# Modulation by row block, the input split from PSUM, and VectorE in place of GpSimd in a hybrid decoder layer

## The chip, the cores and the metric

The kernel runs on one core of a Trainium2 chip. The metric is device time in microseconds (us) of one launch. The engines are TensorE (PE, with its weight loads as PEld), VectorE (DVE), ScalarE (ACT), GpSimd (POOL) and SyncE (SP, which here only issues transfers).

## The reference, cut to what matters

One layer of a decoder with 1024 tokens and 1024 channels, all in float32:

```python
mod = (jax.nn.silu(c) @ w_ada + b_ada)[:, None, :]
shift, scale, gate = jnp.split(mod, 3, axis=-1)
h = rms_norm(x, norm_g) * (1.0 + scale) + shift
(a_q, a_kv, a_g, a_z, b_q, ..., d_z) = jnp.split(h @ w_in, IN_OFFSETS, axis=-1)
y_a = nsa_attention(...)           # three masked softmaxes per head, ALiBi slopes
y_b = banded_attention(...)        # window of 128, a sink per head
y_c = stick_breaking_attention(...)   # suffix sums of log(1 - sigmoid)
y_d = retention(...)
for i, (y, z) in enumerate(branches):
    yi = y.reshape(B, S, BRANCH_W) * jax.nn.silu(z)
    term = jax.nn.sigmoid(h @ w_merge[i]) * (yi @ w_br[i])
    merged = term if merged is None else merged + term
x = x + gate * (merged @ w_out)
return rms_norm(x, final_g)
```

## The kernel before, in words

**Exact products.** A float32 matrix product is made of three matmuls on parts: each operand is split into a high part (`whi`, `hh`, written by an ACT copy) and the rest (`wlo`, `hl`, a subtraction on DVE or POOL). TensorE sums hi*hi, hi*lo and lo*hi in PSUM.

**First stage** (`first_gen`). The eight 128-token tiles of x are loaded (`load_x`) and normalised (`norm_x`: squares and scaling on ACT, a small power on POOL). The shift and scale of the modulation are sums over the 1024 rows of `w_ada`. `load_ada(k)` loads for channel block k (128 channels) all 1024 rows of its shift and of its scale columns, 512 KB each, in pieces of 128 columns, thus 512 bytes each. `mod_k(k)` multiplies each of the eight row blocks by `silc`, which holds silu(c), and adds it up on DVE (`SP<-FA,silc,SP` or `SP<-SP,silc` in the trace, 256 columns an instruction). Two matmuls with a column of ones then sum over the partitions (`t<-SP`), and two small DVE steps write `mod`. `h_k(k, n)` transposes four x tiles into a PSUM bank `t`, has ACT apply scale and shift into a tile `xs` in SBUF (`t<-t,mod`; the pool of that tile is also named t1), has DVE copy it to `hh` and POOL subtract to `hl`. The first half of the tokens (`h0`) is done block by block, and each block's 18 matmuls (six products of `w_in` columns for mixer C, three parts each) follow; `w_in` comes in eight pieces of 384 KB, each split by ACT and POOL. The second half (`h1`) follows at the end. `WARM` is a run of 36 transposes without use for the result, ahead of the first matmuls.

**Mixers.** Units of attention C, D, A, B run between the projections. The softmaxes of A and B subtract a distance table with one DVE instruction that also takes the row's maximum (`mx`), multiply the maximum by the negative slope (`mx<-mx,kbt`), run the exponential on ACT with its row sum (`den`), clamp `den` by one DVE instruction over its two or four columns, invert it, and scale on POOL. Mixer C has a running sum on DVE (`TENSOR_TENSOR_SCAN`) whose unused second input is the tile it also reads first.

**Merge and output.** The gates of `w_merge` use a seven-product scheme on 2x2 blocks (`pair`, `product`, `op`), whose sums of `h` blocks (`td`, T1 to T3) are loaded back from DRAM into `tt`, six loads of 1 MB, ahead of the first two weight tiles' work. The output product uses the same scheme: `w_jobs` and the loops after it prepare the blocks of `w_out` (`wr`), in part on POOL, and write them over the blocks of `h` (`b11`, `b12`, `b21`, `b22`, in the trace `hh` and `hl`), over `yh` and `yl` (`wy`) and over `tt` (`w11`). The last block, `wt4`, takes memory that `wr` held.

**Order.** The instructions of each of four stretches (`with md.noted`) are collected and put in an order by a planner (`Program.schedule`): it simulates the engines with costs written in `cost`, and takes on each engine the ready step with the lowest rank. Tables (`SHIFT_PE`, `SHIFT`) move the rank of labelled steps. It also models that DVE and POOL steps flagged `port` exclude each other. The loops that prepare `b22`, `b12` and `wy` stand outside of the planned stretches. On the chip each engine runs its own list in that order.

All instructions issued through the planner have one line in the trace (L372); L395 marks those issued directly. Tiles are named by their pool: `SP` holds working rows (the modulation's sums, softmax rows), `FA` the x tiles and others, `wst` loaded weights, and PSUM banks are `d`, `s`, `t`, `y`.

Of the kernel before, what the change touches and what calls it, by code (L numbers as in the profile page):

```python
# [16 lines left out]
P = 128  # L17
S = 1024
# [27 lines left out]
def shape_constants():  # L46
# [14 lines left out]
    for h in range(NH):  # L61
        kb[:, KB_IS + h] = 1.0 / SLOPES[h]
# [26 lines left out]
def chunks(w):  # L89
# [22 lines left out]
    ('D1', 7): 19159, ('first', 0): 300, ('first', 2): 0, ('first', 3): 20000, ('first', 4): 3,  # L112
    ('first', 5): 9000, ('first', 6): 10000, ('first', 7): 10300, ('h0', 1): 9967, ('h0', 2): 1000,
    ('h0', 3): -300, ('h0', 4): 10030, ('h0', 5): -10000, ('h0', 6): 300, ('h0', 7): -10100,
    ('h1', 0): 30, ('h1', 1): -10000, ('h1', 4): 0, ('h1', 5): 10000, ('h1', 6): 19960,
    ('h1', 7): 113, ('item', 0): 397, ('item', 12): 19900, ('item', 15): -100, ('item', 16): 10570,
    ('item', 17): 18970, ('item', 19): 10170, ('item', 2): 10000, ('item', 20): 10000,
    ('item', 21): 20003, ('item', 22): 9970, ('item', 23): 10300, ('item', 24): -10,
    ('item', 25): 10013, ('item', 26): 830, ('item', 27): 9697, ('item', 4): -270,
    ('item', 6): -11000, ('item', 7): 10000, ('item', 9): 293, ('mod', 0): 10000, ('mod', 1): 0,  # L120
    ('mod', 4): 370, ('mod', 7): 300, ('out', 102): -10000, ('out', 103): 330, ('out', 106): -10030,
    ('out', 107): 10000, ('out', 109): 0, ('out', 110): 0, ('out', 111): 3000, ('out', 112): 9987,
    ('out', 113): 30, ('out', 114): 10000, ('out', 115): 10000, ('out', 117): -10,
    ('out', 119): -10890, ('out', 120): -30, ('out', 121): 3000, ('out', 122): -10000,
    ('out', 123): 10027, ('out', 124): 294, ('out', 126): -10800, ('out', 128): 10000,
    ('out', 129): 10000, ('out', 94): -407, ('out', 95): -3013, ('out', 96): 9900,
    ('out', 97): -130, ('tile', 0): 320, ('tile', 1): -570, ('tile', 10): -10010, ('tile', 11): 300,
    ('tile', 12): -990, ('tile', 13): 30, ('tile', 14): 3000, ('tile', 15): 10, ('tile', 16): 3000,
    ('tile', 17): 0, ('tile', 18): 10000, ('tile', 19): -9300, ('tile', 2): -100, ('tile', 21): 900,
# [19 lines left out]
    ('ada', 6): 20000, ('ada', 7): 0, ('first', 7): 0, ('h0', 0): 70, ('h0', 1): -9980,  # L149
    ('h0', 2): 12783, ('h0', 3): -7000, ('h0', 5): -1000, ('h0', 7): 0, ('h1', 0): -10000,  # L150
    ('h1', 1): -10000, ('h1', 2): 10200, ('h1', 5): 30, ('h1', 6): -33, ('item', 0): 0,
    ('item', 1): 0, ('item', 10): 400, ('item', 11): 2000, ('item', 12): 9882, ('item', 13): 0,
    ('item', 15): 0, ('item', 16): 320, ('item', 17): 10, ('item', 18): -333, ('item', 19): -10100,
    ('item', 2): 1330, ('item', 20): 20000, ('item', 21): -11000, ('item', 22): 0,
    ('item', 23): -30, ('item', 27): 0, ('item', 29): 30, ('item', 3): 1000, ('item', 30): 10000,
    ('item', 5): 0, ('item', 6): -307, ('item', 8): -200, ('mod', 0): -10000, ('mod', 2): -10130,
    ('mod', 3): 10, ('mod', 4): 300, ('mod', 5): -10930, ('mod', 6): -30, ('mod', 7): 0,
# [33 lines left out]
class Program:  # L191
# [127 lines left out]
    def schedule(self):  # L319
# [17 lines left out]
        while len(order) < len(ops):  # L337
# [89 lines left out]
def hybrid_kernel(ctx: ExitStack, tc: tile.TileContext, x, c, w_ada, b_ada, norm_g, w_in, cmp_pos,  # L427
# [567 lines left out]
    with ac:  # L995
# [101 lines left out]
        def first_gen():  # L1097
# [5 lines left out]
            for t in range(3):  # L1103
                load_x(t)
# [932 lines left out]
```

## Time and profile before

| | |
|---|---|
| median of 3 runs | 1100.29 us (1096.93 to 1100.64) |
| profiled execution | 1097.74 us, its span 1096.0 us |
| PE busy | 1041.4 us (95% of the span) |
| DVE, ACT, POOL busy | 821.6, 575.7, 490.8 us |
| mean granted clock of TensorE | 0.984 of full speed |
| PE busy share by 40 slices | 3 and 8 tenths in the first two, 9 in all others but the last (6) and two with 7 |

PE is busy nearly all the time, so the profile is read for the stretches in which it is not, and for those in which its granted clock (the column PEclk) is below 1.00; the two levels are 1.2 GHz (0.5) and 2.4 GHz (1.0).

### The profile page before, as it was taken

What the parts mean: (1) busy time and instruction counts of PE and PEld (TensorE: products, weight loads), DVE (VectorE), ACT (ScalarE), POOL (GpSimd) and SP (SyncE); (2) the same over time, 40 slices, a digit from 0 to 9 for tenths busy, and PEclk for the clock granted to TensorE, in tenths of its full rate; (3) what the DMA queues carried; (4) which work ended last, traced back from release to release, by engine and by line L of the source; (5) the groups of instructions that cost most, each with busy time, mean ns of one, the idle gap of its engine ahead of it and who ended that gap; (6) DMA issues with size and microseconds to landing.
All of it is one profiled execution on the core that took longest, in us unless ns stands there. A gap on an engine that the chain in (4) does not pass through costs nothing.

```text
span 1096.0 us, 16030 instructions
## 1 busy us (share of the span) xinstructions
PE 1041.4 (95%) x5391; PEld 874.2 (80%) x5391; DVE 821.6 (75%) x1803; ACT 575.7 (53%) x1265; POOL 490.8 (45%) x519
## 2 busy tenths in 40 slices
PE   3899999999999999999999899999999999997996
PEld 2688787789778888889888688888888888875885
DVE  5868995997467868988997345688796565589897
ACT  4378984896246767677775133333333333254343
POOL 4575214204444466564565122255555555485102
PEclk8899999999999999999999999999999999999998
DMA  9846211013232111232323912332232222261222
GB/s 306 243 134 180 68 39 39 16 26 78 32 78 59 30 49 41 90 110 88 99 85 129 344 49 85 99 94 70 87 87 58 53 79 79 69 232 43 111 98 94
DMA packets 127718, 105.47 MB, mean 96 GB/s; under 512 B 15132, under 2 KB 108372, under 8 KB 126868
## 3 DMA queue, kind: packets, MB, share of 16 engines
q1 hardware_dynamic: 126160, 99.95, 30.5%
q0 software_dynamic: 1408, 4.48, 1.3%
q8 instruction: 42, 0.69, 0.3%
q14 instruction: 40, 0.33, 0.1%
q10 hardware_dynamic: 68, 0.02, 0.0%
HBM read 81.88 MB, written 17.83 MB: 91 GB/s over the span
## 4 chain that ended last, share of the span: by engine, by line
PE 77%; DVE 10%; ACT 4%; DMA 4%; issue 2%; POOL 1%; SPq 1%; POOLq 0%; DVEq 0%; ACTq 0%
PE d L372 30%; PE s L372 22%; PE t L372 15%; PE y L372 9%; DVE SP L372 3%; DMA wst<-in_w_merge_dram 2%; ACT t L372 1%; DVE lo L372 1%; DVE FA L372 1%; ACT SP L372 1%; SPq L372 1%; DVE yl L395 1%; DMA SP<-in_w_ada_dram 1%; DVE acc L372 1%; DMA FA<-in_x_dram 1%
## 5 line engine op out<-in xcount | busy, mean ns | idle before, releaser
L372 POOL TENSOR_TENSOR wlo<-wst,whi 128x512 fp32r<-128x512 f32 (+1 forms) x108 | 145.2, 1354 | 175.3 <-ACT whi L372 173.4
L372 PE MATMUL d<-hh,whi 128*128 128x512 f32 x440 | 181.3, 412 | 1.7 <-ACT whi L372 0.7
L372 ACT ACTIVATE whi<-wst 128x512 fp32r<-128x512 f32 (+2 forms) x121 | 89.2, 740 | 161.2 <-PE s L372 42.7
L372 PE MATMUL d<-hh,wlo 128*128 128x512 f32 x440 | 173.2, 394 | 0.0
L372 PE MATMUL d<-hl,whi 128*128 128x512 f32 x440 | 172.2, 392 | 0.0
L372 PEld LDWEIGHTS d<-hh,wlo 128*128 128x128 f32 x440 | 82.9, 188 | 19.1 <-DVE wlo L372 0.4
L372 ACT ACTIVATE hi<-t 128x512 fp32r<-128x512 f32 (+3 forms) x148 | 74.9, 527 | 38.4 <-PE t L372 34.1
L372 PEld LDWEIGHTS d<-hh,whi 128*128 128x128 f32 x440 | 83.3, 189 | 14.3 <-ACT whi L372 1.1
L372 PEld LDWEIGHTS d<-hl,whi 128*128 128x128 f32 x440 | 83.1, 189 | 10.6
L372 DVE TENSOR_TENSOR lo<-t,hi 128x512 fp32r<-128x512 f32 (+2 forms) x132 | 80.6, 623 | 11.9 <-ACT hi L372 10.9
L372 POOL TENSOR_SCALAR SP<-SP,den,gates 128x640 f32<-128x640 f32 (+7 forms) x64 | 53.0, 837 | 75.1 <-DVE den L372 25.5
L372 PE MATMUL s<-hh,whi 128*128 128x512 f32 x200 | 79.8, 399 | 6.3 <-ACT whi L372 6.3
L372 POOL TENSOR_TENSOR acc<-acc,mt 128x512 f32<-128x512 f32 x44 | 67.2, 1528 | 34.4 <-DVE mt L372 33.6
L372 PE MATMUL s<-hh,wlo 128*128 128x512 f32 x200 | 79.1, 395 | 0.9 <-DVE wlo L372 0.9
L372 PE MATMUL s<-hl,whi 128*128 128x512 f32 x200 | 78.5, 394 | 0.0
L372 PE MATMUL t<-kbt,SP 128*128 128x128 f32 (+1 forms) x470 | 69.5, 273 | 7.4 <-DMA kbt<-in_kb_dram 6.5
L372 ACT ACTIVATE SP<-SP,mx 128x257 f32<-128x257 f32 (+9 forms) x96 | 62.2, 650 | 20.7 <-DVE mx L372 17.0
L372 PEld LDWEIGHTS t<-kbt,SP 128*128 128x128 f32 (+1 forms) x470 | 55.0, 141 | 14.7 <-DMA kbt<-in_kb_dram 6.5
L372 DVE TENSOR_TENSOR mt<-s,mt 128x512 f32<-128x512 f32 x61 | 41.2, 686 | 33.9 <-PE s L372 33.7
L372 PE MATMUL s<-tt,whi 128*128 128x512 f32 x192 | 59.1, 389 | 0.0
L372 ACT ACTIVATE mt<-mt 128x512 f32<-128x512 f32 x56 | 35.2, 630 | 41.4 <-DVE mt L372 41.2
L372 ACT ACTIVATE t<-t 128x512 f32<-128x512 f32 (+5 forms) x97 | 49.9, 523 | 3.7 <-DVE t L372 2.3
(347 smaller groups left out, 2798.3 us busy)
## 6 DMA issues: line engine op xcount, KB each, us to landing
wst<-in_w_merge_dram SPq DMA_DIRECT2D x32, 512.0 KB, 4.3
wst<-in_w_in_dram SPq DMA_DIRECT2D x26, 512.0 KB, 3.9
td<-FA SPq DMA_DIRECT2D x32, 256.0 KB, 2.5
tt<-td SPq DMA_DIRECT2D x6, 1024.0 KB, 12.6
FA<-in_w_ada_dram SPq DMA_DIRECT2D x10, 512.0 KB, 7.1
FA<-in_x_dram SPq DMA_DIRECT2D x8, 512.0 KB, 6.7
pst<-in_w_br_dram SPq DMA_DIRECT2D x32, 128.0 KB, 2.3
ga<-in_w_ada_dram SPq DMA_DIRECT2D x16, 256.0 KB, 3.0
```

The costliest lines, as they stand in the source:

```text
L372: fn(*args, **kw)
L395: return f(*a, **k)
```

## The change

**Modulation.** The eight channel blocks form three groups (blocks 0 and 1, 2 and 3, 4 to 7). A transfer brings one row block (128 rows) of one group, with pieces of 256 columns (1 KB) in the first two groups and 512 columns (2 KB) in the third, into a ring of six 4 KB rows; the loads of x tiles 0 to 3 alternate with those of group 0. DVE sums a group at a time (512 or 1024 columns an instruction), and all of a group's sums over partitions follow. x tiles 4 to 7 are loaded after the third group.

**Input parts.** ACT writes `hh` straight from PSUM and then the full value back to PSUM in a second pass; DVE subtracts from PSUM to `hl`. The copy on DVE and the subtraction on POOL are gone.

**Softmax and scan.** The slope enters in the instruction that takes the extreme (now a minimum of negated scores), so the multiplication of `mx` is gone; the clamp of `den` is one instruction for each column; the scan's second input is in PSUM.

**T loads and w_out.** T2 is loaded first, T3 and T1 after the first weight tile's matmuls were issued. All POOL subtractions of `w_out`'s blocks and of `wt4` are on DVE, and `b22`, `b12`, `wy` are inside the planned stretch.

**Planner.** It adds 88 ns when PE goes from transposes to matmuls. Both tables are new, save for the labels `out` from 102 on, nearly all of `op` from 107 on, and `wt4`.

```diff
+            op.turn |= name == "transpose"
...
+                free[e] += 88.0 * (turned and not op.turn)
+                turned = op.turn
...
+        MG = ((0, 2), (2, 4), (4, 8))
+        macc = [misc[:, 512:1024], misc[:, 512:1024], SP[:, 3, :]]
+        RING = [FA[:, 4], FA[:, 5], FA[:, 6], FA[:, 7], SP[:, 1], SP[:, 2]]
...
+        NEXT = {(0, 1): ((1, 4), (1, 5)), (0, 3): ((1, 6), (1, 7)), (0, 5): ((2, 0),), (0, 7): ((2, 1),), (1, 1): ((2, 2),),
+                (1, 3): ((2, 3),), (1, 5): ((2, 4),), (1, 7): ((2, 5),), (2, 0): ((2, 6),), (2, 1): ((2, 7),)}
...
-        def load_ada(k):
-            for s in range(2):
-                sy.dma_start(AD[k][:, s], w_ada[0].rearrange("(r p) c -> p r c", p=P)[:, :, s * D + k * P:s * D + (k + 1) * P])
+        def load_ada(g, r):
+            k0, k1 = MG[g]
+            sy.dma_start(AD[g, r], w_ada[0, r * P:(r + 1) * P, 0:2 * D].rearrange("p (s c) -> p s c", s=2)[:, :, k0 * P:k1 * P])
...
+        def mod_g(g):
+
+            k0, k1 = MG[g]
+            m = macc[g].rearrange("p (s c) -> p s c", s=2)
+            for r in range(KC):
+                md.label = "mod", 8 * g + r
+                if r == 0:
+                    ve.tensor_scalar(m, AD[g, r], silc[:, 0:1], None, op0=ALU.mult)
+                else:
+                    ve.scalar_tensor_tensor(m, AD[g, r], silc[:, r:r + 1], m, op0=ALU.mult, op1=ALU.add)
+                for gr in NEXT.get((g, r), ()):
+                    md.label = "ada", 8 * gr[0] + gr[1]
+                    load_ada(*gr)
...
-            xs = t1_pool.tile([P, 512], F32, name=f"xs{k}_{n}", tag="t1")
-            se.activation(xs, t, AF.Identity, scale=mod[:, 16 + k:17 + k], bias=mod[:, k:k + 1])
-            ve.tensor_copy(hh[:, k, sl], xs)
-            po.tensor_tensor(hl[:, k, sl], xs, hh[:, k, sl].bitcast(F32), ALU.subtract)
+            for d in (hh[:, k, sl], t):
+                se.activation(d, t, AF.Identity, scale=mod[:, 16 + k:17 + k], bias=mod[:, k:k + 1])
+            ve.tensor_tensor(hl[:, k, sl], t, hh[:, k, sl].bitcast(F32), ALU.subtract)
...
-                                ve.tensor_tensor_scan(ac_[:, ::-1], l[:, ::-1], l, 0.0 if carry is None else carry,
+                                ve.tensor_tensor_scan(ac_[:, ::-1], l[:, ::-1], ps[:, :n], 0.0 if carry is None else carry,
...
-                    ve.tensor_tensor(mx[:, 0:n], mx[:, 0:n], ns[:, 0:n], ALU.mult)
...
-                    ve.tensor_scalar(den[:, 0:n], den[:, 0:n], TINY, None, op0=ALU.max)
+                    for j in range(n):
+                        ve.tensor_scalar(den[:, j:j + 1], den[:, j:j + 1], TINY, None, op0=ALU.max)
...
-            for i, t in ((1, T2), (0, T1), (2, T3)):
+            def t_load(i, t):
                 for v in range(2):
                     sy.dma_start(f(t[v]), td[i, v])
+
+            t_load(1, T2)
             for n, _ in enumerate(run_items(it_m[:2])):
                 md.step += 1
+                if n == 16:
+                    t_load(2, T3)
+                    t_load(0, T1)
...
-                parts(w11, k, r11[:, k], po)
+                parts(w11, k, r11[:, k], ve)
...
-                po.tensor_tensor(r12[:, k], r22[:, k], r12[:, k], ALU.subtract)
+                ve.tensor_tensor(r12[:, k], r22[:, k], r12[:, k], ALU.subtract)
...
-                po.tensor_tensor(t4f[k], r21[:, k], r11[:, k], ALU.subtract)
+                ve.tensor_tensor(t4f[k], r21[:, k], r11[:, k], ALU.subtract)
...
+            wy = [v.rearrange("p k (a c) -> p (k a) c", c=512) for v in (yh, yl)]
+            for n, (d, src, e) in enumerate(((b22, r12, ve), (b12, r21, ve), (wy, r22, ve))):
+                md.label = "w", 33 + n
+                for k in range(4):
+                    parts(d, k, src[:, k], e)
...
-                parts(wt4, k, t4f[k], po)
+                parts(wt4, k, t4f[k], ve)
```

## Rows read from the trace of the kernel before

**Rows 1.** The page's busy times of the engines, whole span.

```profile
PE 1041.4 (95%) x5391; PEld 874.2 (80%) x5391; DVE 821.6 (75%) x1803; ACT 575.7 (53%) x1265; POOL 490.8 (45%) x519
```

**Rows 2.** Busy time by stage: us, engines (instructions), PEclk, DMA share, GB/s.

```profile
0.00:28.00 28.00, 10.43 (x55) 7.69 (x55) 14.96 (x45) 12.52 (x24) 12.79 (x26) 0.87 1.05 306
28.00:31.00 3.00, 3.00 (x9) 2.37 (x10) 3.00 (x5) 1.29 (x2) 3.00 (x3) 0.53 1.15 317
...
45.00:51.00 6.00, 5.42 (x15) 3.94 (x14) 4.38 (x9) 0.47 (x1) 2.88 (x2) 0.50 1.06 349
...
100.00:150.00 50.00, 48.84 (x267) 41.29 (x268) 47.26 (x93) 47.20 (x101) 11.82 (x10) 1.00 0.26 68
...
300.00:340.00 40.00, 36.28 (x203) 30.04 (x203) 24.54 (x102) 20.95 (x64) 17.64 (x31) 1.00 0.32 73
340.00:600.00 260.00, 257.91 (x1533) 223.40 (x1531) 220.24 (x697) 182.72 (x470) 147.02 (x193) 1.00 0.25 78
600.00:620.00 20.00, 20.00 (x90) 16.57 (x89) 5.79 (x11) 2.24 (x4) 3.38 (x4) 1.00 0.97 364
620.00:630.00 10.00, 6.69 (x23) 4.67 (x22) 5.64 (x8) 3.20 (x6) 2.36 (x2) 0.83 0.77 258
...
1000.00:1020.00 20.00, 12.94 (x44) 9.22 (x43) 13.82 (x18) 8.58 (x16) 7.91 (x6) 0.83 0.42 157
```

**Rows 3.** Timeline of the first stage: start, us, engine, instruction, idle before and releaser.

```profile
21.62 1.33 ACT L372 ACTIVATE FA<-FA,ss 128x512 f32<-128x512 f32 x2 [3.96 <-POOL ss L372]
...
27.09 1.01 PE L372 MATMUL t<-SP 128*128 128x1 f32 x4 [2.23 <-DVE SP L372]
27.34 0.42 DVE L372 CAST hh<-t 128x512 fp32r<-128x512 f32 x1
27.96 0.77 PE L372 MATMUL d<-hh,whi 128*128 128x512 f32 x1
...
78.04 0.39 PE L372 MATMUL y<-hh,RA 128*128 128x512 f32 x1
```

**Rows 4.** Waits of PE, whole span: us in total, times, longest us.

```profile
PE t L372 <- DVE SP L372: 6.6, 2, 4.3
...
PE s L372 <- ACT whi L372: 6.3, 1, 6.3
...
PE d L372 <- ACT whi L372: 4.0, 2, 3.3
```

**Rows 5.** Transfers of 17 to 26 us, then of 965 to 975 us.

```profile
DMA packets 5019, 2.64 MB, mean 293 GB/s; under 512 B 80, under 2 KB 4977, under 8 KB 5019
...
DMA packets 2006, 3.80 MB, mean 380 GB/s; under 512 B 64, under 2 KB 191, under 8 KB 2004
```

**Rows 6.** Instructions by form, ACT, 0 to 80 us: busy us, mean ns, idle before.

```profile
L372 ACT ACTIVATE t<-t,mod 128x512 f32<-128x512 f32 x13 | 10.0, 777 | 11.8 <-DVE mod L372 11.1 <-PE t L372 0.5
```

**Rows 7.** Instructions by form, DVE, whole span.

```profile
L372 DVE TENSOR_TENSOR lo<-t,hi 128x512 fp32r<-128x512 f32 x94 | 62.9, 683 | 9.1 <-ACT hi L372 8.2
...
L372 DVE TENSOR_TENSOR_SCAN SP<-t,cy 128x512 f32<-128x512 f32 x12 | 16.5, 1374 | 0.1
...
L372 DVE TENSOR_SCALAR den<-den 128x2 f32<-128x2 f32 x32 | 9.5, 298 | 4.4 <-ACT SP L372 4.2
...
L372 DVE TENSOR_TENSOR mx<-mx,kbt 128x2 f32<-128x2 f32 x32 | 6.9, 217 | 0.1
...
L372 DVE TENSOR_SCALAR ssq<-ssq 128x1 f32<-128x1 f32 x8 | 1.7, 209 | 0.1
```

**Rows 8.** The chain that ended last, from 600 to 625 us: start, us, what.

```profile
603.89 17.80 DMA wst<-in_w_merge_dram
```

**Rows 9.** Timeline around the start of the output product.

```profile
995.71 1.78 DVE L372 TENSOR_TENSOR acc<-acc,mt 128x512 f32<-128x512 f32 x1
...
1009.49 2.19 ACT L372 ACTIVATE wt<-wst 128x512 fp32r<-128x512 f32 x4 [2.11 <-DVE yl L395]
...
1012.25 0.79 PE L372 MATMUL s<-hh,whi 128*128 128x512 f32 x1 [6.34 <-ACT whi L372]
```

More of the change, by code (lines that the diff above doesn't have):

```diff
@@ L118 @@
[L118 to L129, printed above, removed]
@@ new lines @@
+    ('out', 126): -10800, ('out', 128): 10000, ('out', 129): 10000, ('out', 94): 0,
+    ('out', 95): -10, ('out', 96): 10303, ('out', 97): -13, ('sum', 1): 9900, ('sum', 2): -10000,
+    ('tile', 0): -9700, ('tile', 1): 3936, ('tile', 10): -10030, ('tile', 11): -9727,
+    ('tile', 13): 10000, ('tile', 14): 0, ('tile', 15): -370, ('tile', 16): -10000,
+    ('tile', 17): 9700, ('tile', 18): -10400, ('tile', 19): 0, ('tile', 21): -100,
+    ('tile', 25): 10600, ('tile', 26): 9970, ('tile', 27): -400, ('tile', 28): 0,
@@ L133 @@
+    ('tile', 29): 11000, ('tile', 3): -10000, ('tile', 30): 10030, ('tile', 31): 63,
+    ('tile', 4): 20000, ('tile', 5): 10300, ('tile', 6): -10000, ('tile', 7): 1000,
     ('tile', 9): -10000,
@@ L166 @@
-    ('out', 119): 30, ('out', 120): 10970, ('out', 121): -10030, ('out', 122): 3000,
-    ('out', 123): 0, ('out', 124): 30, ('out', 126): -10, ('out', 129): 9990, ('out', 93): -10000,
-    ('out', 94): 10, ('out', 95): 0, ('out', 96): 300, ('split', 0): -10300, ('split', 1): -960,
-    ('split', 3): -9897, ('split', 4): 20000, ('split', 5): -10000, ('split', 6): -10100,
-    ('split', 7): 9200, ('sums', 0): 9633, ('sums', 1): 10390, ('sums', 2): 10307,
-    ('sums', 3): 18717, ('tile', 15): -10, ('tile', 23): -9900, ('tile', 31): 10,
[5 rows of a table removed]
[12 rows of a table added]
@@ L177 @@
+    ('split', 0): 0, ('split', 1): 30, ('split', 2): 9700, ('split', 3): 1000, ('split', 4): -10300,
+    ('split', 5): 0, ('split', 6): -100, ('sum', 0): 0, ('sum', 1): 0, ('sums', 0): 9700,
+    ('sums', 1): 10097, ('sums', 2): 2057, ('tile', 15): 19630, ('tile', 23): -1300,
[5 rows of a table added]
 }
@@ L181 @@
 class Op:
-    __slots__ = ("eng", "calls", "dur", "lat", "preds", "succs", "prio", "start", "step", "size", "port", "narrow")
+    __slots__ = ("eng", "calls", "dur", "lat", "preds", "succs", "prio", "start", "step", "size", "port", "narrow", "turn")
     def __init__(self, eng, prio, step):
@@ L1065, in norm_x @@
                     se.activation(xg, xg, AF.Copy, scale=ss[:, 3:4])
-        def mod_k(k):
-            m = macc[k % 2]
-            for q in ((0,), (1,)) if k == 0 else ((0, 1),):
-                q = slice(q[0], q[-1] + 1)
-                for r in range(KC):
-                    w = AD[k][:, q, r, :]
-                    if r == 0:
-                        ve.tensor_scalar(m[:, q], w, silc[:, 0:1], None, op0=ALU.mult)
-                    else:
-                        ve.scalar_tensor_tensor(m[:, q], w, silc[:, r:r + 1], m[:, q], op0=ALU.mult, op1=ALU.add)
-            pm = pools["t"].tile([P, 512], F32, name=f"pm{k}", tag="t")
+        def mod_g(g):
[10 more added lines that the diff above has]
+                    load_ada(*gr)
+            md.label = "sum", g
+            pm = pools["t"].tile([P, 512], F32, name=f"pm{g}", tag="t")
             yield
+            n = k1 - k0
             for s in range(2):
-                te.matmul(pm[:, s:s + 1], lhsT=m[:, s, :], rhs=one, start=True, stop=True)
-            ve.tensor_tensor(mods[:, :, k], pm[:, 0:2], bias[:, :, k], ALU.add)
-            ve.scalar_tensor_tensor(mod[:, 16 + k:17 + k], mod[:, 8 + k:9 + k], 1.0, cols[:, 8 + k:9 + k], op0=ALU.add, op1=ALU.mult)
+                for k in range(n):
+                    te.matmul(pm[:, s * n + k:s * n + k + 1], lhsT=m[:, s, k * P:(k + 1) * P], rhs=one, start=True, stop=True)
+            ks = slice(k0, k1)
+            ve.tensor_tensor(mods[:, :, ks], pm[:, 0:2 * n].rearrange("p (s k) -> p s k", s=2), bias[:, :, ks], ALU.add)
+            ve.scalar_tensor_tensor(mod[:, 16 + k0:16 + k1], mod[:, 8 + k0:8 + k1], 1.0, cols[:, 8 + k0:8 + k1], op0=ALU.add, op1=ALU.mult)
         def h_k(k, n):
@@ L1102, in first_gen @@
             po.dma_start(posr.rearrange("r (j d) -> r j d", j=2), cmp_pos[0].rearrange("j r d -> r j d"))
-            for t in range(3):
+            for t in range(4):
                 load_x(t)
-            load_ada(0)
-            load_x(3)
-            st.dma_upto(1)
-            load_ada(1)
-            load_ada(2)
+                for r in (2 * t, 2 * t + 1):
+                    load_ada(0, r)
+            st.dma_upto(2)
+            for r in range(4):
+                load_ada(1, r)
             po.memset(mhalf, -0.5)
@@ L1134, in grow @@
                 ws[k] = it_first.w
-                md.label = "mod", k
-                yield from mod_k(k)
-                for j in {0: (3,), 1: (4,), 2: (5,), 3: (6,), 5: (7,)}.get(k, ()):
-                    md.label = "ada", j
-                    load_ada(j)
-                for t in {4: (6, 7), 6: (4, 5)}.get(k, ()):
+                for g, (k0, k1) in enumerate(MG):
+                    if k0 == k:
+                        yield from mod_g(g)
+                for t in {4: (4, 5, 6, 7)}.get(k, ()):
                     md.label = "x", t
@@ L1892, in hybrid_kernel @@
                 pass
-        wy = [v.rearrange("p k (a c) -> p (k a) c", c=512) for v in (yh, yl)]
-        for k in range(4):
-            parts(b22, k, r12[:, k], ve)
-        for k in range(4):
-            parts(b12, k, r21[:, k], po)
-        for k in range(4):
-            parts(wy, k, r22[:, k], ve)
+            wy = [v.rearrange("p k (a c) -> p (k a) c", c=512) for v in (yh, yl)]
[3 more added lines that the diff above has]
+                    parts(d, k, src[:, k], e)
         rstack.close()
```

94 lines of the change are left out of this document (52 added, 42 removed), and 74 rows, old and new, of tables (SHIFT, SHIFT_PE).

## Prediction

> **What bounds the kernel now.** I read the page's busy times first: PE is busy 1041.4 of 1096.0 us [rows 1], so 54.6 us without matmuls is nearly all that can be had unless PE's own work changes. The view of busy time by stage then says where those microseconds lie [rows 2], and PE's waits and the timeline say on what they end [rows 3, 4, 8, 9]. The reader should compare PE's busy time with the stage's length, and its matmul count with that of an undisturbed stage: 600 to 620 us holds 90 matmuls of full width in 20 us, 222 ns each.
>
> Three places stand out. (1) The first stage: until 27.96 us PE has only transposes and small sums [rows 3]; the eight channel blocks then run until 78.04 + 0.2 = 78.3 us, with one wait of 4.3 us for the modulation's sum [rows 4] and two stretches at half clock (0.53 and 0.50), in which 9 and 15 matmuls ran where 13.5 and 27 fit [rows 2]. (2) 620 to 630 us: 23 matmuls where 45 fit. The chain there is one transfer of a `w_merge` tile, 17.80 us from issue to landing [rows 8]. (3) 1000 to 1020 us: 44 where 90 fit, 10.2 us lost, 6.34 of them one wait [rows 2, 9]. What is left is the tail after the last matmul, which the change doesn't touch, and small waits: 3.7 us in 300 to 340, 2.1 us in 340 to 600 [rows 2].
>
> **The first stage, term by term.** Work inside 27.96 to 78.3: 50.3 us, less the wait of 4.3, less (13.5 - 9) x 0.222 = 1.0 and (27 - 15) x 0.222 = 2.7 for the clock, leaves 42.3 us at full speed. I put 19 of it on the first four blocks and 23 on the last four, which have most of the second half's transposes beside them.
>
> When can it start? Before the first matmul the change needs x tiles 0 to 3 (2.10 MB), group 0 (2.10), one piece of `w_in` (0.39) and about 0.3 of constants: 4.9 MB. At the 306 GB/s of the first 28 us, start-up included [rows 2], it is in at 16.0 us. Behind it come one 512-column sum step (0.68, as a subtraction of that size [rows 7]), four sums over partitions (1.01 us for two at low clock [rows 3], so 2.0), two small DVE steps with their hops (estimated 0.8) and one ACT pass (0.78 [rows 6]): 20.3 us. If the last x tile's scaling waits for POOL as now (3.96 us [rows 3]), 24.3. I take 22. The old path lost more: `hh` had to pass DVE, whose copy stood behind the next block's sums and came at 27.34 [rows 3]; now ACT writes `hh`.
>
> Length of pieces: 512-byte pieces moved 293 GB/s and transfers with 1.9 KB a packet 380 [rows 5]. No row has 1 KB; I take the middle, 337. Group 1 with two `w_in` pieces is 2.88 MB, 8.6 us, landed at 24.6, before PE needs it. Group 2 is 4.19 MB, with two to five `w_in` pieces 4.98 to 6.16 MB, 13.1 to 16.2 us: 37.7 to 40.8. A 1024-column step (2 x 0.68), eight sums (2.0 to 4.0), small steps 0.8 and ACT 0.78 put the fifth block's first matmul at 42.6 to 47.8; I take 45. The first four blocks end at 22 + 19 + 1 (half clock at the start) = 42. So PE waits 3 us for group 2; I add 1.4 for the clock, half of what the old wait cost, and end at 45 + 23 + 1.4 = 69.4 us, 8.9 before 78.3.
>
> That needs ACT. The second pass is 16 x 0.777 = 12.4 us more [rows 6], of which twelve fall after 42 us, beside the norms of x tiles 4 to 7; and from 100 to 150 us ACT is busy 47.2 of 50 us [rows 2]. PE has projections to run meanwhile, so I give back 1 us: **-8**. Bounds: best, a start at 20.3, no wait and no half clock, 62.6: about -15. Worst, everything at 293 GB/s (group 2's sum ready near 51) and the full 2.7 of clock: 76.7, -1.6; or the second half's eight extra passes (6.2 us) all delay PE: -2. The hidden `hl` costs nothing: DVE's subtraction from PSUM is 0.68 [rows 7] against a copy and a POOL subtraction in series.
>
> At this point the Trainium skill, "DMA: Bandwidth & Descriptors", section Specifications, speaks against the change: it gives 512 bytes as the least transfer that runs at line rate, so longer pieces would bring nothing. By that rule the term is that of the worst case above. The 293 against 380 GB/s of this trace does not agree with it.
>
> **T loads.** Six loads of 1 MB stand in SP's queue ahead of the `w_merge` tile. With only T2's two there, about 2.1 MB at 380 GB/s (5.5 us) precede it and the 4.2 MB of T3 and T1 (11 us) come behind; T3 is first read by the third of the seven products, two of 12 x 0.222 = 2.7 us after some 620, so at 625 or later; issued by about 606, soon after the tile's 603.89, both are in by 617. The stage's loss, 22 matmuls x 0.222 = 4.9 us, goes nearly whole: **-4.5**; bounds -4.9 and 0 (the planner may still place T3 and T1 ahead of the tile).
>
> **w_out's blocks.** The wait before 1012.25 ends on an ACT pass that stands behind `wt4`'s four; those waited for the last DVE read of `wr` [rows 9], because `wt4` lies in its memory. Nothing in the change moves `wt4` back, and the ranks of the products from 102 on stay. So what counts is when DVE is through. `b12` and `b22` overwrite `h` and can't start before the last gate tile is through PE, at about the first step of [rows 9]. From there DVE gains the end of contention: four sums in a row beside POOL's work took 1.66 to 1.78 us (the first is [rows 9]) instead of 0.68, 4.1 us back. It loses `b12`'s four, 2.7. DVE ends some 1.4 us earlier, and the first sums that PE awaits come earlier too: **-2**. Bounds: the wait and its half clock vanish wholly, -10; or DVE, already 13.82 of 20 us busy there [rows 2], also delays other steps: +3.
>
> **Softmax, scan, planner.** In the 32 units with two columns the product of `mx` (217 ns) and the clamp (298) become two single-column clamps (at most 209 each [rows 7]; at least nothing): DVE gains 0.1 to 0.5 us in each, 3 to 16 us in all. The sixteen units with four columns trade one clamp and one product for four clamps, at worst two more instructions, +6.7. Either way it is hidden: in 340 to 600 DVE has 40 us free and PE lacks 2.1 [rows 2]; without that cover it would be 7 us. The scan took 1374 ns [rows 7]; reading PSUM could let it run free of POOL or lengthen it, and mixer C's PE loss is a few waits. PE lacks 1.2, 3.7 and 2.1 us in the three stretches of [rows 2] between 100 and 600; the reordered tables can remove these 7.0 or add two stalls like that of 300 to 340: -7 to +7, I take **-1**.
>
> **Sum.** -8 - 4.5 - 2 - 1 = -15.5. The profiled execution took 1097.74 us (1.74 around its span); that gives 1082.2. It lies 2.6 below the median shown (1100.29, of 1096.93 to 1100.64), so I forecast **1083 us**.
>
> **Rivals.**
> *The output product's wait closes* (18 in 100). If DVE, no longer slowed by POOL, finishes before PE is through product 103, PE goes on at full clock: 8 us more, 1075. For it: DVE's slowed instructions; against it: `wt4` still stands first on ACT.
> *The start gives little* (15 in 100): the rate stays at 293 GB/s, or the second ACT pass delays PE: -2 instead of -8, 1089. The skill's rule above is the first of these; I give that part 5 of the 15, for the trace speaks against it.
> *The T order changes nothing* (8 in 100), the tile staying behind all loads: 1087.5.
> *DVE becomes the bound at w_out: slower* (6 in 100). Twenty POOL subtractions come to DVE in this stage, which has 6.2 us free in 1000 to 1020 [rows 2]. If each takes the mean of 0.68 and the slowed 1.78 [rows 7, 9], they are 24.6 us, and PE stands still for some 18.4 more: 1097.7 - 13.5 + 18.4 = 1102.6, and at 1.78 each 1113.6. It decides from some 19 us of delay on. Against it: the slowing came beside POOL's work, which leaves this stage.
> *The new order costs PE 6 to 12 us between 80 and 600* (6 in 100): 1090 to 1096.
> My forecast has the other 47.
>
> **The numbers.** 1083 is the likeliest case, its own range 1077 to 1088. To leave out no more than 2 in 10, the range must take in the closed wait together with a start near its best bound (1069) and the small start together with an untouched T order (1094): **1069 to 1094**. A measurement here tells about 0.5% (5.5 us) from no change: faster is below 1094.8. Nearly all of the first three cases and of the fourth lie there; the reordering is half, the DVE case none, and two of the small gains failing together takes a little more: faster 0.84, same 0.10, slower 0.06.
>
> **What would show it.** After: the first matmul on `hh` near 22 us and the eighth block's last near 70, with a PE wait of about 3 us in between that ends on the third group's sum; transfers above 320 GB/s while the groups load; no gap at 620 (less the shift of some 8 us); a wait of 4 to 6 us before the output product, still on ACT behind `wt4`; ACT near full from 45 to 75 us after the start. I am wrong if group 2 lands after 48 us, if ACT is what PE waits for in the first 150 us, if the wait at the output product is gone or doubled, or if new waits of more than 6 us appear between 80 and 600.

## The result and the profile after

The changed kernel takes 1079.71 us (median of 4 runs, 1079.27 to 1081.45) against 1098.65 us before (median of 4, 1096.93 to 1100.64). The ratio is 0.9826, 95% interval [0.9806, 0.9847]: 1.7% faster. The profiled execution took 1079.71 us, its span 1077.9. A second batch with the unedited changed kernel (e11 below) gave 0.9820 [0.9804, 0.9836].

The page's busy times, the answer to [rows 1]:

```profile
PE 1040.4 (97%) x5391; PEld 873.4 (81%) x5391; DVE 796.5 (74%) x1797; ACT 584.4 (54%) x1281; POOL 435.5 (40%) x483
```

TensorE's work is the same, 1.0 us less of it. VectorE lost 25.1 us and GpSimd 55.3; ScalarE gained 8.7. So 17.1 of the 18.1 us of span are time in which TensorE stood still and no longer does. To place them I read the same five marks in the timeline of every kernel: the first matmul on `hh`, the start of the eighth channel block's last matmul, of the first gate tile after attention, of the first product on T1 to T3, and of product 102.

| us | first on hh | eighth block's last | to first gate tile | to first T product | to product 102 | to the end |
|---|---|---|---|---|---|---|
| before | 27.96 | 78.04 | 515.32 | 31.35 | 374.99 | 96.30 |
| after | 21.78 | 69.85 | 511.86 | 28.27 | 375.35 | 92.57 |
| difference | -6.18 | -8.19 | -3.46 | -3.08 | +0.36 | -3.73 |

The first two columns are times from the span's start, the others lengths of stretches; the last five differences add up to -18.1. In the runs below a stretch that an edit leaves alone comes out at 511.1 to 514.3 us (to the first gate tile), 27.9 to 28.3 (to the first T product), 373.0 to 375.4 (to product 102) and 91.2 to 92.7 (to the end), one profile each. So 3 us in the first of these, 2.4 in the third and 1.5 in the last mean nothing by themselves. The -3.46 is read as some 1 to 4 us, and even that with care, for the kernel before has one profile alone.

Busy time by stage, the answer to [rows 2]:

```profile
0.00:28.00 28.00, 14.79 (x73) 11.74 (x74) 17.19 (x32) 14.47 (x27) 11.36 (x23) 0.88 0.97 340
...
31.00:40.00 9.00, 6.59 (x29) 5.12 (x28) 7.82 (x11) 3.92 (x6) 3.37 (x3) 0.85 0.95 340
...
51.00:70.00 19.00, 19.00 (x101) 15.66 (x99) 5.88 (x9) 18.84 (x31) 10.18 (x11) 1.00 0.54 158
100.00:150.00 50.00, 49.47 (x275) 41.11 (x274) 47.68 (x88) 45.57 (x92) 13.71 (x13) 1.00 0.29 69
285.00:325.00 40.00, 38.36 (x202) 31.46 (x200) 22.59 (x81) 17.84 (x46) 14.68 (x22) 1.00 0.23 60
325.00:580.00 255.00, 253.62 (x1511) 218.37 (x1510) 212.22 (x735) 180.38 (x472) 143.57 (x193) 1.00 0.25 76
600.00:620.00 20.00, 19.78 (x87) 15.73 (x86) 10.00 (x15) 5.44 (x10) 4.45 (x4) 1.00 0.97 321
```

The gap after 620 us is gone. TensorE lacks 0.5, 1.6 and 1.4 us in the three attention windows, where it lacked 1.2, 3.7 and 2.1. ScalarE is busy 18.84 of 19 us from 51 to 70, and TensorE 19.00 of 19 beside it: full, but not what TensorE waits for. What is left of the first stage's loss is the half clock of the first matmuls (granted 0.50 until 27 us) and 31 to 40 us. Its matmuls, from the timeline (the answer to [rows 3]):

```profile
21.78 0.80 PE L380 MATMUL d<-hh,whi 128*128 128x512 f32 x1 [1.77 <-ACT hh L380]
...
32.98 0.95 PE L380 MATMUL t<-SP 128*128 128x1 f32 x8
...
35.25 0.51 PE L380 MATMUL d<-hh,RW 128*128 128x512 f32 x1 [0.41 <-ACT hh L380]
37.50 0.80 PE L380 MATMUL d<-hl,RW 128*128 128x512 f32 x1 [1.74 <-DVE hl L380]
...
44.08 1.84 PE L380 MATMUL t<-SP 128*128 128x1 f32 x16
...
49.76 0.39 PE L380 MATMUL d<-hh,whi 128*128 128x512 f32 x1
...
69.85 0.40 PE L380 MATMUL y<-hh,RA 128*128 128x512 f32 x1
```

TensorE waits at the second group, group 1 of the prediction, not at the third. (A sum over partitions is two records in the trace, so x8 at 32.98 are the four sums of the second group and x16 at 44.08 the eight of the third.) Behind the sums of 32.98, which TensorE takes up without having waited, it stands 0.26, 0.41 and 1.74 us. The third group's sums are done while blocks three and four still run, and the fifth block follows at 49.76 without a wait. What ends the wait of 1.74 us, on ScalarE and VectorE:

```profile
34.42 1.45 ACT L380 ACTIVATE hh<-t,mod 128x512 fp32r<-128x512 f32 x2 [3.96 <-DVE mod L380]
35.76 1.42 ACT L380 ACTIVATE t<-t,mod 128x512 f32<-128x512 f32 x2
...
35.56 1.28 DVE L380 SCALAR_TENSOR_TENSOR SP<-FA,silc,SP 128x1024 f32<-128x1024 f32 x1
36.76 0.68 DVE L380 TENSOR_TENSOR hl<-t,hh 128x512 fp32r<-128x512 f32 x1
```

ScalarE writes `hh` of both blocks before the second pass of either, which ends at 36.51 for the first; VectorE comes free of a sum of the third group at 36.8. So `hl` waits for both, within 0.3 us of each other.

The `w_merge` tile, from the chain of waits (the answer to [rows 8]), and SP's issues around it:

```profile
591.59 15.00 DMA wst<-in_w_merge_dram
```

```profile
588.49 2.46 SPq L380 DMA_DIRECT2D tt<-td  x5
...
591.59 0.46 SPq L380 DMA_DIRECT2D wst<-in_w_merge_dram  x1
...
601.29 0.46 SPq L380 DMA_DIRECT2D tt<-td  x1
```

Five of the six T loads still go ahead of the tile, not two. And around the output product (the answer to [rows 9]):

```profile
990.48 2.19 ACT L380 ACTIVATE wt<-wst 128x512 fp32r<-128x512 f32 x4 [2.75 <-DVE hl L380]
...
993.24 0.80 PE L380 MATMUL s<-hh,whi 128*128 128x512 f32 x1 [2.99 <-ACT whi L380]
```

It is the same wait as before, on the same ScalarE pass behind the same four passes of `wt4`, 2.99 us long instead of 6.34.

### The profile page after: what moved, and what is told of

It reads as the page before. It is cut to its first block, busy times and chain, and to the rows that moved or that the text cites. A ratio compares the mean times of both kernels' runs of the same rounds, so it can differ in the third digit from the quotient of the medians.

```text
span 1077.9 us, 16022 instructions
## 1 busy us (share of the span) xinstructions
PE 1040.4 (97%) x5391; PEld 873.4 (81%) x5391; DVE 796.5 (74%) x1797; ACT 584.4 (54%) x1281; POOL 435.5 (40%) x483
## 4 chain that ended last, share of the span: by engine, by line
PE 70%; DVE 11%; ACT 6%; issue 5%; DMA 5%; POOL 2%; SPq 1%; POOLq 0%; ACTq 0%; DVEq 0%
PE d L380 25%; PE s L380 22%; PE t L380 14%; PE y L380 8%; DVE SP L380 4%; ACT t L380 2%; DVE lo L380 1%; DMA wst<-in_w_merge_dram 1%; DVE t L380 1%; ACT SP L380 1%; ACT whi L380 1%; DVE FA L380 1%; POOL RA L380 1%; DMA RA<-RA 1%; ACT hi L380 1%
## 5 line engine op out<-in xcount | busy, mean ns | idle before, releaser
L380 PEld LDWEIGHTS d<-hl,whi 128*128 128x128 f32 x440 | 83.5, 190 | 11.6 <-DVE hl L380 0.4
```

Source lines behind the costliest of these rows:

```text
L380: fn(*args, **kw)
```

## The experiments

Each run is given with its median and its ratio to the kernel before, which ran beside it (medians 1097.65, 1100.54 and 1098.98 us in the three batches). The stretches named are those of the table above.

**e1: shorter rows.** Every transfer of a `w_ada` piece is split by channel block.

```diff
-sy.dma_start(AD[g, r], src)
+for k in range(k1 - k0):            # one plan entry, k1 - k0 transfers
+    nc.sync.dma_start(dst[:, :, k*P:k*P+P], src[:, :, k*P:k*P+P])
```

> The changed kernel with every piece of `w_ada` moved in rows of 512 bytes instead of 1 KB (groups 1, 2) and 2 KB (group 3); same bytes, same order of all engines, more transfers issued. If the rate of the pieces matters, as the prediction's middle of 293 and 380 GB/s says: the first group's 2.1 MB take 1.3 us longer (7.2 us at 293 GB/s against 5.9 at 357), so the first matmul on hh comes at 23 to 24 instead of 21.78 us; all 8.4 MB take about 6 us longer, the third group's sum comes after 48 instead of 45.96 and the fifth block waits for it; the eighth block's last matmul at 72 to 75 instead of 69.85; total 1082 to 1085 against 1079.7. If 512 bytes move at the same rate as longer rows: first matmul within 0.4 us of 21.78, total within 1 us of 1079.7.

1084.76 us, 0.9883 [0.9861, 0.9905]: 5 us back. First matmul on hh at 24.10, the eighth block's last at 79.61. The windows 28 to 38 us of the changed kernel, of e1 and of the kernel before (last columns: share of DMA time, GB/s):

```profile
28.00:38.00 10.00, 7.59 (x37) 6.07 (x36) 8.78 (x11) 3.69 (x6) 5.81 (x4) 0.96 1.02 369
```

```profile
28.00:38.00 10.00, 9.06 (x42) 7.30 (x41) 7.59 (x11) 1.89 (x3) 3.29 (x4) 0.91 0.94 270
```

```profile
28.00:38.00 10.00, 10.00 (x45) 8.23 (x46) 9.37 (x20) 3.25 (x4) 5.89 (x5) 0.86 1.14 303
```

Rows of 512 bytes move 270 to 303 GB/s at a DMA share near or above 1, rows of 2 KB 369. In e1 alone the number of issues could also count: twelve of 128 KB took SP 6.45 us, 244 GB/s. The kernel before moved 512-byte rows in 512 KB transfers and reached 303, so the length of the rows goes with about a fifth of the rate; e1 doesn't separate the rest. The delay of 9.8 us is larger than the transfers' own, for VectorE works in order. Its timeline in e1:

```profile
46.94 1.28 DVE L380 SCALAR_TENSOR_TENSOR SP<-FA,silc,SP 128x1024 f32<-128x1024 f32 x1 [3.45 <-DMA FA<-in_w_ada_dram]
48.14 0.68 DVE L380 TENSOR_TENSOR hl<-t,hh 128x512 fp32r<-128x512 f32 x1
```

A sum of the third group waits for its piece, and the `hl` that TensorE needs now stands behind it. Of the 9.8 us 6.2 reach the span; the rest is made up in the stretches behind, 2.3 of it to product 102 (373.03 us here against 375.35, both ends of what other runs show there), so it is scatter as far as I can tell.

The Trainium skill, "DMA: Bandwidth & Descriptors", section Specifications, gives 512 bytes as enough for line rate; this trace doesn't agree (303 GB/s at 512 bytes, 369 at 2 KB, same queue and stage).

**e2: h made the old way.**

```diff
-for d in (hh[:, k, sl], t):
-    se.activation(d, t, AF.Identity, scale=..., bias=...)
-ve.tensor_tensor(hl[:, k, sl], t, hh[:, k, sl], ALU.subtract)
+se.activation(xs, t, AF.Identity, scale=..., bias=...)
+ve.tensor_copy(hh[:, k, sl], xs)
+po.tensor_tensor(hl[:, k, sl], xs, hh[:, k, sl], ALU.subtract)
```

> The changed kernel with h made as before: one ScalarE pass into SBUF, hh by a VectorE copy, hl by a GpSimd subtraction. If the old path was what delayed the start (the copy stands in VectorE's queue behind modulation sums): first matmul on hh 1.5 to 3 us later (23.5 to 25 instead of 21.78), a similar delay again at the third block, total 1082 to 1086. If the earlier start came from the order of the loads and the size of the first group alone: first matmul before 22.7, total within 1.5 us of 1079.7, perhaps below, since ScalarE has 16 passes (12.4 us) less.

1102.53 us, 1.0034 [1.0018, 1.0050]: all of the gain lost, and more than expected. First matmul on hh at 25.37, 3.6 us later, and the wait before it (3.04 us) ends on VectorE's copy, which stands between sums and is slowed itself:

```profile
23.18 0.74 DVE L380 SCALAR_TENSOR_TENSOR SP<-SP,silc 128x512 f32<-128x512 f32 x1
23.84 1.48 DVE L380 CAST hh<-t 128x512 fp32r<-128x512 f32 x1
```

The eighth block ends at 83.28, 13.4 us later. Another 13.1 us are lost between there and the first gate tile (524.95 against 511.86 us), where the edit has only the last two tiles of `h` (to 88 us): the planner, given another list of instructions, lays attention out anew with tables made for another one. So e2 shows that the old path costs the start 3.6 us; how much of the 13.4 us is its own and how much the plan's, it doesn't.

**e3: the tile behind all six T loads.**

```diff
+md.label = None                      # rank of the loads: none between them
 t_load(1, T2); t_load(2, T3); t_load(0, T1)
 for n, _ in enumerate(run_items(it_m[:2])):
-    if n == 16: t_load(2, T3); t_load(0, T1)
```

> The changed kernel with all six loads of T1 to T3 issued ahead of the `w_merge` tile (it now stands behind five), nothing else moved on TensorE. If the tile's place in the queue closed the gap: one more load of 1 MB (2.8 us at 380 GB/s) ahead of it, tile landed about 2.8 us later, TensorE's wait there 0.2 -> 2.5 to 3.3 us and half clock behind it, total 1083 to 1084. If the gap closed for another reason (the loads began 11.6 us earlier, TensorE reached the place only 10.6 us earlier, other waits took its place): wait below 1.2 us, total 1079 to 1081.

1084.33 us, 0.9877 [0.9854, 0.9900]. The chain's transfer and TensorE's waits behind it:

```profile
593.79 17.95 DMA wst<-in_w_merge_dram
```

```profile
614.77 0.73 PE L380 MATMUL d<-tt,whi 128*128 128x512 f32 x2 [3.37 <-ACT whi L380]
616.66 0.79 PE L380 MATMUL d<-tt,wlo 128*128 128x512 f32 x1 [1.16 <-DVE wlo L380]
```

One load of 1 MB makes the tile's 15.00 us 17.95, as its size at 380 GB/s says (2.8), and the gap of before is back: 31.41 us to the first T product (before 31.35, after 28.27) and some 2 us more behind it (377.35 against 375.35). The first theory holds.

**e4: the blocks back on GpSimd.** Five `ve` of the diff become `po` again, their places in the program kept. The planner orders this stage anew with them: 33 of TensorE's 5391 matmuls and 20 of ScalarE's instructions change places between 945 and 991 us, six of the matmuls from ahead of product 102 to behind its start.

> The changed kernel with the twenty subtractions of w_out's blocks given back to GpSimd, their places in the planned stretch kept. If VectorE's contention with GpSimd was the cost: VectorE's sums beside them take 1.6 to 1.8 us again instead of 0.69, the wait before the output product grows from 2.99 to 5 to 6.3 us, total 1082 to 1085. If what helped was that b22, b12 and wy are planned with the tiles now: the wait stays within 1 us of 2.99, total within 1 us of 1079.7.

1087.52 us, 0.9906 [0.9878, 0.9934], 7.8 us more than the changed kernel and more than either theory gave. Product 102 to the end takes 100.79 us (the six matmuls among them, 1.3 us of work at full clock), longer than before's 96.30. VectorE and GpSimd in the timeline:

```profile
982.85 1.74 POOL L380 TENSOR_TENSOR wst<-wr,wr 128x512 f32<-128x512 f32 x1
983.36 1.78 DVE L380 TENSOR_TENSOR wlo<-acc,whi 128x512 fp32r<-128x512 f32 x1
984.55 5.11 POOL L380 TENSOR_TENSOR hl<-wr,hh 128x512 fp32r<-128x512 f32 x3
985.06 5.75 DVE L380 TENSOR_TENSOR hl<-wr,hh 128x512 fp32r<-128x512 f32 x4
```

VectorE's subtraction, 0.69 us in the changed kernel, takes 1.1 to 1.8 beside GpSimd's; the one of 983.36 ends 0.55 us after GpSimd's has. TensorE waits 3.57 us for a gate sum at 991.47 and 4.35 us at 998.75. The first theory holds in its mechanism: VectorE's steps are slow again and TensorE waits behind them. How much of the 7.8 us is the new order's, e4 doesn't say.

The Trainium skill, "SBUF — State Buffer", section Who interferes with whom, says that a VectorE instruction with two SBUF inputs contends with a GpSimd instruction that reads SBUF. The rows agree: from 964 to 968 us, beside GpSimd, VectorE's steps with one input in PSUM stay at 0.68 to 0.69 us, and the subtractions between them take 1.13 to 1.19.

**e10: the last three blocks behind the planned stretch,** as before, but on VectorE.

```diff
-for n, (d, src, e) in enumerate(((b22, r12, ve), (b12, r21, ve), (wy, r22, ve))):
-    md.label = "w", 33 + n
+for d, src in ((b22, r12), (b12, r21), (wy, r22)):     # behind the plan
```

> The changed kernel with the last three w_out blocks issued behind the planned stretch, as before, but still on VectorE. If VectorE's freedom from GpSimd made the gain at w_out and not the planning: product 102's start to the end stays within 1.5 us of 92.6 us. If the planning was needed: the last block comes later behind the stage's last sums, the wait before product 106 grows from 2.99 to 5 us or more, and 102 to the end takes 95 us or more, near the 96.3 of the kernel before.

1080.56 us, 0.9834 [0.9815, 0.9853], against 1078.80 of the unedited kernel in its batch. Product 102 to the end takes 93.88 us (92.57 and 91.80 unedited), and the wait is

```profile
994.67 0.79 PE L380 MATMUL s<-hh,whi 128*128 128x512 f32 x1 [4.82 <-ACT whi L380]
```

Unedited, the wait is 2.99 us in each of the other runs that leave this order alone. So most of the gain over the kernel before (96.30 us) is VectorE's, free of GpSimd; the planning adds 1 to 2 us.

**e5 and e12: product 106 in turn.** In the changed kernel TensorE's table puts 106 into the middle of 103, where it waits for the pass behind `wt4`.

```diff
 SHIFT_PE = { ...
-    ('out', 106): -10030,
```

> The changed kernel with one entry of TensorE's table left out, so that product 106 comes after 104 and 105 instead of between the third and the fourth step of 103; the planner re-plans only this last stage. If TensorE's wait of 2.99 us there (and 0.25 us behind it) is only the place of 106, whose ScalarE pass stands behind wt4's four, which wait for VectorE: 103 and 104 have their operands by 991, the wait falls below 0.5 us, the half clock of 993 to 999.9 us goes too (some 3 us), total 1073 to 1075 against 1079.7. If VectorE's own lateness is the bound (it is busy without a gap to 995.4 us): the wait moves to 104 or 105, 2 to 3 us long, total 1079 to 1081.

> e5 again, beside the unedited changed kernel. If the earlier product 104 is worth what the trace of e5 says (product 102's start to the end 90.6 us instead of 92.6; TensorE's last matmul 3.8 us earlier, half of it lost again to VectorE): 1.5 to 2.5 us below the changed kernel of this batch. If the 2 us were chance: no difference.

1079.30 us, 0.9807 [0.9787, 0.9827]; and in the last batch 1076.90 us, 0.9801 [0.9785, 0.9817], beside 1078.80 us, 0.9820, of e11. Neither theory of e5 holds whole: the wait is gone, as the first said, and the total is the second's. (The planner orders the output product anew: 123 matmuls change places.) TensorE's last matmul comes 3.8 us earlier after product 102 (79.1 against 82.9 us), but the end only 2.0. The chain that ended last, from 1040 us on, by line, of the changed kernel and of e5:

```profile
by line: PE s L380 27.9%; PE t L380 16.9%; PE d L380 14.0%; DVE mt L380 10.6%; DVE z L380 5.5%; issue 4.2%; POOLq L2056 2.6%; ACT mt L380 1.9%; ACT z L380 1.9%; POOL ssq L380 1.4%; DVE ssq L380 0.6%; ACTq L380 0.0%
```

```profile
by line: DVE mt L380 28.3%; DVE z L380 15.7%; issue 12.9%; DVE wlo L380 11.6%; POOL ssq L380 5.2%; DVE acc L380 4.9%; POOLq L2056 2.6%; ACT mt L380 1.9%; ACT z L380 1.9%; DVE s L380 1.6%; DVE ssq L380 1.2%; POOLq L380 0.1%; ACTq L380 0.0%
```

With the wait closed, VectorE is the bound of the output product; a new wait of TensorE at 1028 us (1.73) ends on its `wlo`. It was near it before: in e11 VectorE is busy 62.28 of the 64 us from 1002 on. e12 is the fastest kernel here, 1.9 us below the changed one in its batch, though the intervals overlap.

> The changed kernel itself, unedited, as the reference of this batch: its ratio to the kernel before again 0.981 to 0.985; the stretch from the eighth block to the first gate tile 511 to 515 us if the 2.4 us by which e5's was longer came from the chip and not from its edit.

e11 is the reference of that batch: 511.88 us from the eighth block to the gate tile, 91.80 at the end.

**e8: e5, and ScalarE's next operands ahead of the block r11.**

```diff
+first = [i for i, o in enumerate(md.ops) if o.eng == "act" and o.label in (("op", NP), ("op", NP + 1))]
+for o in md.ops:
+    if o.eng == "act" and o.label[0] == "w" and o.label[1] < 4: o.preds.update(first)
```

> The changed kernel with product 106 in turn (as e5) and, in the stage before, ScalarE's passes over the w_out block r11 held behind those of the next two operands, so that TensorE's waits of 0.88 and 0.67 us at 946 to 948 us and the half clock to 953 us (some 2 us) should go; nothing of the work is left out. If both waits are only orders on ScalarE: 1070 to 1073. If the second edit only delays VectorE's block sums and the wait comes back behind it: as e5, 1074 to 1077.

1079.25 us, 0.9816 [0.9797, 0.9836]: no better than e5 (1079.30). TensorE waits 1.53 us at 949 us, and ScalarE in front of it 7.21 us for the `w_merge` tile itself, which is issued at 941.90 right behind 1 MB of `w_out` and lands at 948.64. The order on ScalarE was not the cause.

**e6: the clamps twice.** Each clamp of `den` is issued two times, nothing re-planned.

```diff
+md.ops[-1].calls *= 2
```

> The changed kernel with each of the 128 clamps of den issued twice in place, the plan and every other order unchanged: 128 x 0.148 = 18.9 us more on VectorE between 100 and 580 us, where the change had removed about 7 us. If softmax's VectorE steps are hidden, as the prediction said: total within 1.5 us of 1079.7. If they stand on the path: a part of the 18.9 us shows, 3 us or more, and the 7 us removed would then explain the 2.5 us by which this stretch gained more than forecast.

1090.15 us, 0.9915 [0.9896, 0.9935], some 10 us more than the unedited kernel. By form on VectorE, and the largest new wait of TensorE from 70 to 600 us:

```profile
L380 DVE TENSOR_SCALAR den<-den 128x1 f32<-128x1 f32 x256 | 36.5, 150 | 8.5 <-ACT SP L380 3.4
```

```profile
PE s L380 <- DVE mx L380: 3.3, 9, 1.2
```

The clamps' 17.3 us became 36.5; the stretch from the eighth block to the gate tile grew from 511.9 to 523.6. In its own batch e5 and e8 show 514.3 and 513.8. So about half of VectorE's 19.2 added us come out at the end. That the softmax steps are hidden is wrong, at least under the changed kernel's order.

**e7: the old softmax and scan, re-planned.** All of the diff on softmax, sinks and scan is undone.

> The changed kernel with softmax and the scan as before (product of mx with the slopes, one clamp over all columns, the scan's second operand from SBUF); the planner re-plans with tables that belong to another list of instructions. If the plan decides and not the steps: the stretch from the eighth block to the first gate tile, 511.9 us long now, grows by 3 to 13 us with waits spread over many names (e2's re-plan grew it by 13), while VectorE's busy time grows by only 5 to 8 us. If the steps decide: it grows by at most 7 us, and the new waits end on mx, den, cy or the scan's SP. If neither: within 2 us.

1127.58 us, 1.0252 [1.0235, 1.0269]; the stretch takes 559.97 us. TensorE's waits from 70 to 640 us:

```profile
PE t L380 <- POOL SP L380: 6.1, 6, 1.7
PE s L380 <- DVE SP L380: 5.5, 6, 1.7
PE s L380 <- DVE mx L380: 4.5, 9, 1.1
```

The same steps took 515.32 us in the kernel before, under tables of their own. So tables that belong to another list of instructions cost some 45 us (the planner's 88 ns is another difference, of unknown weight).

**e9: the old costs under the new plan.** No order changes; one clamp over all columns and a step of the old product's shape stand before the reciprocal (the old product stood ahead of the exponential), and the scan reads SBUF again. In short:

```diff
-den clamps, one column each
+calls of the reciprocal: clamp den[:, 0:n]; tensor_tensor(den[:, 0:n], ...); reciprocal
-scan(ac_, l, ps[:, :n], ...)
+scan(ac_, l, l, ...)
```

> The changed kernel, its plan and every order kept, with the old steps' work put back in their places: in each softmax unit one clamp over all columns and one product-sized step over the same columns stand before the reciprocal instead of the single-column clamps, and the scan takes its second operand from SBUF again. VectorE gets about 7 us (softmax) and 2.5 us (scan) of work more. If those steps' time is what the stretch from the eighth block to the first gate tile gained (e6 gave back half of its 18.9 us): the stretch grows by 3 to 5 us over that of the changed kernel in this same batch. If the new tables made the gain: by less than 1 us, and e7's 46 us is the order alone.

1093.42 us, 0.9949 [0.9930, 0.9968]: 14.6 us more than e11. The stretch takes 527.07 us, 15.2 more. By form on VectorE, the changed kernel (the answer to [rows 7]) and e9:

```profile
L380 DVE TENSOR_SCALAR den<-den 128x1 f32<-128x1 f32 x128 | 17.3, 148 | 7.4 <-ACT SP L380 5.8 <-ACT cs L380 0.4
L380 DVE TENSOR_TENSOR_SCAN SP<-t,cy,s 128x512 f32<-128x512 f32 x12 | 15.3, 1276 | 0.2
```

```profile
L380 DVE TENSOR_TENSOR_SCAN SP<-t,cy 128x512 f32<-128x512 f32 x12 | 16.1, 1345 | 0.2
L380 DVE TENSOR_SCALAR den<-den 128x2 f32<-128x2 f32 x32 | 9.5, 296 | 3.1 <-ACT SP L380 2.7
L380 DVE TENSOR_TENSOR den<-den,kbt 128x2 f32<-128x2 f32 x32 | 5.9, 185 | 1.1
```

Over the whole span VectorE is busy 17.9 us more than in e11 (813.7 against 795.8), and most of it shows. TensorE has the same 5391 matmuls in the same order in both, so they can be set side by side: e9 falls 3.4 us behind e11 up to 300 us, where the scans are, and another 11.7 from 320 to 580, where the softmaxes are. (e6, set beside e11, loses nothing up to 320 us and 11.6 behind it.)

The means hide what the old steps cost. The shortest, median and longest of all clamps, in ns, of the changed kernel and of e9:

```profile
L380 DVE TENSOR_SCALAR den<-den x128: 123/150/155, 320.5 to 556.9; 128x1 f32<-128x1 f32 x128
L380 DVE TENSOR_SCALAR den<-den x48: 147/170/1248, 325.5 to 572.4; 128x2 f32<-128x2 f32 x32, 128x4 f32<-128x4 f32 x16
```

A clamp over two or four columns takes 147 to 170 ns in the 24 cases in which GpSimd stands still, no more than one over a single column; in the other 24 it takes up to 1248. The single-column clamps take at most 155, though GpSimd runs beside 57 of the 128. The scan is alike (those of 512 columns with a carried sum): 1274 to 1901 ns beside GpSimd with both inputs in SBUF (e9), 1271 to 1281 with one in PSUM. So by these rows what the new steps save is not work but the cases in which VectorE is held up beside GpSimd. No run has the old steps with GpSimd kept away, so that this is all of the 15 us is not shown.

With the order fixed, the new steps are worth about 15 us; e7, with steps of the same kind in another order, takes 33 us more than e9. Between the kernels the stretch gained only 1 to 4, so the order in which the kernel before did it suited its steps better than the new order would suit the old ones. What the new steps would take under the old order was not tried.

## Why the prediction was right, and where its steps failed

The total, 1083 us, was 3.3 us too high, and the case it rested on came true: an earlier start, no gap at the T loads, the output product's wait shorter but not gone. Step by step:

**First stage, -8: measured -8.2, but several of its terms failed and cancel, which is luck.** The first matmul was put at 22 us and came at 21.78; the eighth block was to end at 69.4 and ended at 70.1. In between the prediction had 19 us of work and 1 for the clock in the first four blocks, 3 of waiting and 1.4 of clock at the third group, and 23 for the last four. The last four took 20.3 us. The split into 19 and 23 was wrong, and the trace of before could have told: there the fifth block's first matmul on `hh` comes 19.8 us ahead of 78.3,

```profile
58.53 0.47 PE L372 MATMUL d<-hh,whi 128*128 128x512 f32 x1
```

The way from the first matmul to the fifth block took 28.0 us instead of 24.4: 2.4 of waiting, some 4.2 for two stretches at half clock (to 27.0 and from 37.2 to 40.7 us), and 21.4 of work. The step that failed about the wait is "landed at 24.6, before PE needs it". The second group's last piece landed at 24.9, but its sums ended on VectorE only at 31.2: they are eight steps of 0.7 to 1.5 us, in one queue with `hl` and with the third group's steps of up to 2.0 us, and I had counted only the last step of each group. TensorE took them up at 32.98 with little left to do that doesn't hang on them. There "The hidden `hl` costs nothing" failed too: the longest wait, 1.74 us, ends on `hl`, behind ScalarE's second pass and VectorE's queue alike. That an earlier sum would have let the planner avoid the wait is likely, but no run shows it. The rate of the 1 KB pieces, taken as 337 GB/s, was low: 361 from 2 to 20 us, x tiles among them. That ScalarE would be full was right (18.84 of 19 us from 51 to 70); that it holds nothing up is right there, not at 35 to 37 us.

**T loads, -4.5: measured -3.1 at the gap, -2.7 with the products behind it.** The step "With only T2's two there" is wrong: the planner issues five loads ahead of the tile. One load less was enough, because the wait was just about one load long: e3's one more brings back 3.1 us at the gap and about 2 behind it. The size was near, by a mechanism that I had stretched too far.

**w_out, -2: measured -3.7.** The place, the releaser and the reason (VectorE free of GpSimd) were right, as e4's rows and e10 show; the term was mis-sized, and the wait of 4 to 6 us that was to remain is 2.99. VectorE was to be through 1.4 us earlier. `wt4` began 9.79 us after product 102 before and 5.15 after: 4.6 us earlier. The subtractions run at 0.69 us nearly without a gap, where I had freed four of them from the slowing.

**Softmax, scan and planner, -1: measured -3.5 (1 to 4 with the scatter), and the reason was wrong.** "Either way it is hidden: in 340 to 600 DVE has 40 us free" fails at e6 and e9: with 97 us of idle VectorE time from 100 to 580 in the changed kernel, half (e6) to most (e9) of its added time still reaches the end. The prices failed as well: 217 and 298 ns [rows 7] are means over steps of 0.13 to 0.17 us and a few that were held up to 1.3 us beside GpSimd, and it is where those few stand that counts. Free time of an engine is no cover when its steps stand in the chain that TensorE waits for next and both queues are in a fixed order. The bounds of -7 to +7 held, by luck: how much of the gain is the steps' and how much the tables' stays open.

**The rival that the wait closes** was priced at 8 us more. e12 closes it for 1.9 us, because VectorE is the next bound.

## What to carry to other kernels

Idle time of an engine hides work only where the work's place in the order has slack: to test it, double the work in place with the plan held, and see what comes out. Read the shortest and the longest of a group of instructions beside its mean: a mean over steps that run free and steps that are held up is the price of neither. When a wait at one engine is closed, price the gain up to the next engine's limit in that stage, read from its busy time there, not by the length of the wait. Count the steps that an in-order engine does between a transfer's landing and its use, not only the last of them.

## What the runs showed of the hardware that I had not expected

- The changed kernel waits 0.88 and 0.67 us at 946 to 948 us, and the granted clock is 0.57 from 948 to 952 us. The same kernel run again (e11) waits 0.95 and 0.69 at the same place, and the clock stays at 1.00. Half clock after short waits is not certain either way.
- 128x512 subtractions from SBUF take VectorE 0.69 us alone and up to 1.78 beside GpSimd's (e4). GpSimd loses too: its sums for `acc` take 1.28 to 1.29 us while VectorE stands still and up to 1.76 beside it (e11; shortest, median and longest in ns):

```profile
L380 POOL TENSOR_TENSOR acc<-acc,mt x44: 1281/1672/1762, 700.8 to 965.3; 128x512 f32<-128x512 f32 x44
```

- A VectorE clamp over one column is never held up by GpSimd here (at most 157 ns in e6, 119 of 256 beside it), one over two or four columns by as much as 1.2 us.
